# Strassen's seven products in the last down projection of a two-block transformer kernel

## Chip, cores and metric

One Trainium2 chip, one of its cores. The time is device microseconds of one execution of the whole program, median of several runs; lower is better.

## What is computed

The reference is a two-layer transformer block (attention, convolutional feed-forward, layer norms) followed by a second block with two branches (attention and a state-space scan). All in float32, 512 tokens, width 1024. The change touches only the last feed-forward of the second block, width `D_FF_2` = 2816:

```
gate, up = jnp.split(h2 @ w_gate_up[i], 2, axis=-1)
ffn = (jax.nn.silu(gate) * up) @ w_down[i]
x = x + rms_norm(ffn, norm2_post[i])
```

The output is x, 512 x 1024.

## The kernel before

Every float32 matrix product is made of three products of a reduced type (`F32R`): each operand is split into a rounded part and the rest (`hi`, `lo`), and hi x hi, hi x lo and lo x hi are summed in PSUM. A split is one ScalarE copy (L185 or L193) and one VectorE subtraction (L186 or L194). `wchunk` does it for weights: a DMA of 512 KB on SP's queue into one of 3 raw tiles, then whi and wlo in one of 4 buffers each.

The last feed-forward, `ffn2`, keeps the normalized input transposed (`xTh`, `xTl`, 8 tiles of 128 rows by 512 tokens). `w_in(g)` computes group g of eleven: 256 columns of gate and of up, as two pairs of products (`ws_pairs`, L217 to L219), each 24 matmuls of 512 columns into one bank of the PSUM pool `mm` (3 banks; `at` has 4). ScalarE takes the Silu of gate (L1410), VectorE multiplies with up (L1411), and the result, 128 hidden units by 512 tokens, is split into `hh` and `hl`, so that hidden units lie on partitions.

The down projection (`xs`, L257 to L259) uses these as the stationary operand: for each of 4 row blocks t (128 tokens) and each half c of the 1024 output columns it sums over hidden tiles. It is done in two parts, as 12 pairs of `hh` and `hl` are kept: groups 0 to 5 by `w_in`, then hidden tiles 0 to 10 into `acc` by ScalarE (`first`), then groups 6 to 10 and tiles 11 to 21 (`second`). `second` adds to `acc` (L1425), takes the mean square on ScalarE (L1429), multiplies with the norm's gain (L1430); with the second half it forms 1/sqrt by a power on GpSimd (`rstd2`, L1385), scales and adds x on VectorE (L1435) and stores the rows from SP's queue (L1436). In the last column half the four last weight chunks are loaded ahead (`stagger`), so that the row blocks end one after the other.

The order of the instructions on each engine is set at build time by a scheduler in the framework; each engine then works in that order, and waits by semaphores.

Of the kernel before, what the change touches and what calls it, by code (L numbers as in the profile page):

```python
# [8 lines left out]
F32 = mybir.dt.float32  # L9
F32R = mybir.dt.float32r  # L10
AF = mybir.ActivationFunctionType
ALU = mybir.AluOpType
# [3 lines left out]
S = 512  # L16
D = 1024
P = 128
KD = D // P
NT = S // P  # L20
# [60 lines left out]
class K:  # L81
# [1297 lines left out]
    def rstd2(self, ss, eps=RMS_EPS):  # L1379
# [5 lines left out]
        nc.gpsimd.tensor_tensor(out=r, in0=v, in1=self.mhalf[:, :1], op=ALU.pow)  # L1385
        return r

    def to_T2(self, src, t):
        for half in range(2):
            pt = self.psa()  # L1390
            for j in range(4):
                self.nc.tensor.transpose(pt[:, j * P:(j + 1) * P], src[half][:, j * P:(j + 1) * P], self.ident)
            sl = slice(t * P, (t + 1) * P)
            self.split(pt.rearrange("p (j c) -> p j c", j=4), self.xTh[:, half * 4:half * 4 + 4, sl], self.xTl[:, half * 4:half * 4 + 4, sl])

    def ffn2(self, pool):
        nc, I = self.nc, self.I
        W1, W2 = I["w_gate_up_2"][0], I["w_down_2"][0]
        G = self.bcast(I["norm2_post_2"][0], "G", pool)
        x = pool.tile([P, NT, D], F32, name="x2")  # L1400
        acc = pool.tile([P, NT, D], F32, name="acc")
        xd = self.xd.rearrange("(t p) d -> t p d", p=P)
        hT = {}

        def w_in(g):
            gc = self.ws_load(W1, g * 256)
            uc = self.ws_load(W1, DFF + g * 256)
            for i, gp, up in self.ws_pairs(gc, uc, g == 0):
                sg = pool.tile([P, S], F32, tag="cy", name="cy", bufs=3)
                nc.scalar.activation(sg, gp, AF.Silu)  # L1410
                nc.vector.tensor_tensor(out=sg, in0=up, in1=sg, op=ALU.mult)  # L1411
                hT[g * 2 + i] = (pool.tile([P, S], F32R, tag="hh", name="hh", bufs=12), pool.tile([P, S], F32R, tag="hl", name="hl", bufs=12))
                self.split(sg, *hT[g * 2 + i])

        def first(c):
            return lambda t, ps: nc.scalar.activation(acc[:, t, c * 512:(c + 1) * 512], ps, AF.Copy)

        sst = [self.sm.tile([P, 2], F32, tag="ss3", name="ss3") for _ in range(NT)]
        ags = {}

        def second(c):
            def epi(t, ps):
                sl = slice(c * 512, (c + 1) * 512)
                a = acc[:, t, sl]
                nc.vector.tensor_tensor(out=a, in0=ps, in1=a, op=ALU.add)  # L1425
                jk = pool.tile([P, 512], F32, tag="jk", name="jk")
                ag = pool.tile([P, 512], F32, tag="ag", name="ag", bufs=6)
                ags[t, c] = ag
                nc.scalar.activation(jk, a, AF.Square, scale=1.0 / 32, accum_out=sst[t][:, c:c + 1])  # L1429
                nc.vector.tensor_tensor(out=ag, in0=a, in1=G[:, sl], op=ALU.mult)  # L1430
                if c == 1:
                    r = self.rstd2(sst[t])
                    for i in range(2):
                        sl = slice(i * 512, (i + 1) * 512)
                        nc.vector.scalar_tensor_tensor(out=x[:, t, sl], in0=ags[t, i], scalar=r, in1=x[:, t, sl], op0=ALU.mult, op1=ALU.add)  # L1435
                        nc.sync.dma_start(self.out[t * P:(t + 1) * P, sl], x[:, t, sl])  # L1436
            return epi

        for g in range(6):
            w_in(g)  # L1440
        for t in range(NT):
            nc.scalar.dma_start(x[:, t, :], xd[t])
        for k0, epi, st in ((0, first, 0), (11, second, 4)):
            if k0:
                for g in range(6, 11):
                    w_in(g)
            for c in range(2):
                self.xs(W2, c * 512, 512, 11, lambda k: hT[k0 + k][0], lambda k: hT[k0 + k][1], epi(c), stagger=st if c else 0, k0=k0)

    def run(self):  # L1450
        nc, I, tc = self.nc, self.I, self.tc
# [72 lines left out]
```

## Time and profile before

| | |
|---|---|
| median of 3 runs | 2114.72 us (2114.29 to 2115.11) |
| profiled execution: its time | 2114.72 us |
| profiled execution: its span, first to last instruction | 2112.5 us |
| mean granted TensorE clock | 0.997 of full speed |
| TensorE, VectorE, ScalarE, GpSimd busy | 98%, 62%, 48%, 3% |

In the rows PE is TensorE (PEld its weight loads), DVE VectorE, ACT ScalarE, POOL GpSimd, SP the queue from which most DMAs are issued. L186 is line 186. Up to L1386 the lines of both kernels are the same; of later ones L1392, L1410, L1411, L1416, L1425, L1429, L1430, L1435 and L1436 belong to the kernel before, and L1397 to L1400, L1413, L1438 to L1482, L1507, L1508 and L1523 to L1534 to the changed one. A listed matmul overlaps the next one: its duration is not what one costs. A row of a timeline gives start, duration, engine, line, operation, output and input, count, and in brackets the idle time before it and what ended it.

### The profile page before, as it was taken

How to read it: one execution, taken by the hardware profiler on the slowest of the kernel's cores; microseconds unless marked ns; L12 is line 12 of the kernel's file. 1: busy time of each engine (PE TensorE's matmuls, PEld its weight loads, DVE VectorE, ACT ScalarE, POOL GpSimd, SP SyncE). 2: the span in 40 equal slices, each digit the busy share in tenths (PEclk: the TensorE clock that was granted, in tenths of full speed). 3: DMA queues.
4: the chain of work that ended last, by engine and by line, in shares of the span. 5: the costliest groups of instructions: out<-in, count | busy, mean ns of one | idle time of the engine just before them, and what ended most of it. 6: DMA issues, size and time to landing. Idle time of an engine off the chain costs nothing.

```text
span 2112.5 us, 27971 instructions
## 1 busy us (share of the span) xinstructions
PE 2068.1 (98%) x10707; PEld 1749.6 (83%) x10707; DVE 1312.0 (62%) x2466; ACT 1018.7 (48%) x1856; POOL 72.5 (3%) x109
## 2 busy tenths in 40 slices
PE   8999999999999999999999998999999999999998
PEld 7888888888888789888888887887898878888887
DVE  6777876535636888775536547897798554332334
ACT  4777554324425977444324434676575343223222
POOL 0000000000000000110000001000000010000000
PEclk9999999999999999999999999999999999999999
DMA  6221233232323121162323333211323425232322
GB/s 168 61 61 61 71 122 116 91 99 80 110 79 100 61 70 61 52 166 84 105 85 111 94 100 98 70 31 35 105 61 90 149 94 176 80 105 89 116 90 70
DMA packets 197563, 193.70 MB, mean 92 GB/s; under 512 B 9029, under 2 KB 170550, under 8 KB 197430
## 3 DMA queue, kind: packets, MB, share of 16 engines
q1 hardware_dynamic: 191494, 173.04, 27.4%
q0 software_dynamic: 4928, 15.22, 2.4%
q10 hardware_dynamic: 1008, 3.67, 0.5%
q8 instruction: 84, 1.38, 0.3%
q14 instruction: 49, 0.40, 0.1%
HBM read 185.61 MB, written 6.29 MB: 91 GB/s over the span
## 4 chain that ended last, share of the span: by engine, by line
PE 51%; DVE 3%; ACT 1%; issue 1%; POOL 1%; POOLq 0%; DVEq 0%; ACTq 0%
PE mm L217 10%; PE mm L218 10%; PE mm L219 10%; PE mm L258 2%; PE mm L257 2%; PE mm L259 2%; PE at L257 2%; PE at L259 2%; PE at L258 2%; PE mm L292 1%; PE mm L293 1%; PE mm L291 1%; PE at L1184 1%; PE at L401 1%; DVE wlo L186 1%
## 5 line engine op out<-in xcount | busy, mean ns | idle before, releaser
L186 DVE TENSOR_TENSOR wlo<-raw,whi 128x1024 fp32r<-128x1024 f32 (+3 forms) x336 | 397.6, 1185 | 337.8 <-ACT whi L185 332.0
L217 PE MATMUL mm<-xTh,whi 128*128 128x512 f32 (+1 forms) x1584 | 605.1, 382 | 0.2 <-ACT xTh L193 0.2
L219 PE MATMUL mm<-xTh,wlo 128*128 128x512 f32 (+1 forms) x1584 | 604.3, 382 | 0.1
L218 PE MATMUL mm<-xTl,whi 128*128 128x512 f32 (+1 forms) x1584 | 604.3, 382 | 0.0
L185 ACT ACTIVATE whi<-raw 128x1024 fp32r<-128x1024 f32 (+3 forms) x336 | 345.2, 1031 | 492.7 <-PE at L259 227.2
L219 PEld LDWEIGHTS mm<-xTh,wlo 128*128 128x128 f32 x1584 | 298.3, 188 | 55.9 <-DVE wlo L186 0.3
L217 PEld LDWEIGHTS mm<-xTh,whi 128*128 128x128 f32 x1584 | 298.4, 188 | 55.0 <-ACT xTh L193 0.5
L218 PEld LDWEIGHTS mm<-xTl,whi 128*128 128x128 f32 x1584 | 298.7, 189 | 54.5 <-DVE xTl L194 0.2
L838 DVE SCALAR_TENSOR_TENSOR cy<-mm,cols,cy 128x511 f32<-128x511 f32 (+1 forms) x172 | 128.5, 747 | 107.7 <-ACT cy L836 104.8
L292 PE MATMUL mm<-wlo,xTh 128*128 128x256 f32 x416 | 117.8, 284 | 0.8 <-DVE wlo L186 0.8
L291 PE MATMUL mm<-whi,xTh 128*128 128x256 f32 x416 | 118.1, 285 | 0.3 <-ACT xTh L193 0.3
L293 PE MATMUL mm<-whi,xTl 128*128 128x256 f32 x416 | 117.5, 283 | 0.2 <-DVE xTl L194 0.2
L257 PE MATMUL mm<-whi,hh 128*128 128x512 f32 x264 | 102.9, 390 | 0.0
L257 PE MATMUL at<-whi,hh 128*128 128x512 f32 x264 | 102.8, 389 | 0.0
L258 PE MATMUL at<-wlo,hh 128*128 128x512 f32 x264 | 102.8, 389 | 0.0
L258 PE MATMUL mm<-wlo,hh 128*128 128x512 f32 x264 | 102.8, 389 | 0.0
L259 PE MATMUL mm<-whi,hl 128*128 128x512 f32 x264 | 102.8, 389 | 0.0
L259 PE MATMUL at<-whi,hl 128*128 128x512 f32 x264 | 102.7, 389 | 0.0
L836 ACT ACTIVATE cy<-mm,cols 128x512 f32<-128x512 f32 x86 | 66.2, 769 | 72.6 <-PE mm L219 72.6
L193 ACT ACTIVATE hh<-cy 128x512 fp32r<-128x512 f32 x66 | 41.1, 623 | 116.5 <-DVE cy L1411 58.9
L193 ACT ACTIVATE ph<-at 128x512 fp32r<-128x512 f32 (+3 forms) x128 | 58.6, 474 | 55.1 <-PE at L401 41.3
L292 PEld LDWEIGHTS mm<-wlo,xTh 128*128 128x128 f32 x416 | 79.4, 191 | 1.9 <-DVE wlo L186 1.0
(416 smaller groups left out, 3432.0 us busy)
## 6 DMA issues: line engine op xcount, KB each, us to landing
raw<-in_ffn_w_in_dram SPq DMA_DIRECT2D x88, 512.0 KB
raw<-in_w_gate_up_dram SPq DMA_DIRECT2D x44, 512.0 KB
raw<-in_ffn_w_out_dram SPq DMA_DIRECT2D x40, 512.0 KB
raw<-in_w_in_dram SPq DMA_DIRECT2D x40, 512.0 KB
raw<-in_a_w_in_dram SPq DMA_DIRECT2D x22, 512.0 KB
raw<-in_w_down_dram SPq DMA_DIRECT2D x20, 512.0 KB
raw<-in_kv_w_dram SPq DMA_DIRECT2D x16, 512.0 KB
raw<-in_a_w_out_dram SPq DMA_DIRECT2D x8, 512.0 KB
```

Source lines behind the costliest of these rows:

```text
L185: nc.scalar.activation(hi, raw, AF.Copy)
L186: nc.vector.tensor_tensor(out=lo, in0=raw, in1=hi.bitcast(F32), op=ALU.subtract)
L217: mm(o, wh, a, start=(k == 0), stop=False)
L218: mm(o, wh, b, start=False, stop=False)
L219: mm(o, wl, a, start=False, stop=(k == ktiles - 1))
L257: mm(o, a, hi[:, kk, :], start=(k == 0), stop=False)
L258: mm(o, a, lo[:, kk, :], start=False, stop=False)
L259: mm(o, b, hi[:, kk, :], start=False, stop=(k == ktiles - 1))
L291: mm(o, a, hi[:, kk, :], start=(k == 0 and t % 2 == 0), stop=False)
L292: mm(o, a, lo[:, kk, :], start=False, stop=False)
L293: mm(o, b, hi[:, kk, :], start=False, stop=(k == ktiles - 1 and t % 2 == 1))
L838: nc.vector.scalar_tensor_tensor(out=y[:, o:], in0=ps[:, :S - o], scalar=self.c1(f"cw{l}{j}", m), in1=y[:, o:], op0=ALU.mult, op1=ALU.add)
```

## The change

Ten of the eleven groups of the down projection go by Strassen's algorithm, in the form of Winograd. Two groups (four hidden tiles) make a phase, `st_phase`. The 512 x 1024 output is a 2 x 2 matrix of blocks of 256 tokens by 512 columns; of each group the hidden tile 0 and 1 are the two halves of the inner dimension. Four blocks of the weight, `b11`, `b12`, `b21`, `b22`, each 128 x 512 for both groups of the phase in one tile of 1024 columns, are loaded unsplit into `wr` (`st_load`). Seven products replace eight: their stationary operands are three of the four blocks of activations and four sums (`st_operands`, VectorE, lines L1397 to L1400, in `R`, split as 256 and 1536 columns), their moving operands `b11`, `b21`, `b22` and four differences formed on GpSimd (L1451, L1452, L1453, L1462), which overwrite `b11`, `b12` and twice `t2`. A product is 12 matmuls of 512 columns (L1438) into two banks, one of each row block, after a split of its weights. The products are added up in `u2`, `u3`, `u5` (VectorE L1464, L1465; ScalarE L1455, L1474) and in `acc`, by VectorE from PSUM (L1471, L1479, L1482) and by GpSimd from SBUF (L1447, L1476). Group 10 goes the usual way (`xsn`), with both column halves of a row block one after the other, and its epilogue ends the program; x is loaded in two buffers instead of four.

```diff
         nc.gpsimd.tensor_tensor(out=r, in0=v, in1=self.mhalf[:, :1], op=ALU.pow)
         return r
 
+    BLOCKS = 7 * 256
+    def st_operands(self, pool, R):
+        tt = self.nc.vector.tensor_tensor
+        b = lambda i: R[:, i * 256:(i + 1) * 256]
+        tt(out=b(4), in0=b(1), in1=b(3), op=ALU.add)
+        tt(out=b(5), in0=b(4), in1=b(0), op=ALU.subtract)
+        tt(out=b(6), in0=b(0), in1=b(1), op=ALU.subtract)
+        tt(out=b(7), in0=b(2), in1=b(5), op=ALU.subtract)
+        hi = pool.tile([P, self.BLOCKS], F32R, tag="hh", name="hh", bufs=3)
+        lo = pool.tile([P, self.BLOCKS], F32R, tag="hl", name="hl", bufs=3)
+        self.split(R[:, 0:256], hi[:, 0:256], lo[:, 0:256])
+        self.split(R[:, 512:2048], hi[:, 256:], lo[:, 256:])
+        return hi, lo
+    def st_load(self, pool, W, g, bufs):
+        Wv = W.rearrange("(g i p) (j c) -> i j p g c", i=2, p=P, j=2)
+        B = {}
+        for i, j in ((0, 0), (0, 1), (1, 1), (1, 0)):
+            B[i, j] = pool.tile([P, 1024], F32, tag="wr", name="wr", bufs=bufs)
+            self.nc.sync.dma_start(B[i, j].rearrange("p (g c) -> p g c", g=2), Wv[i, j][:, g:g + 2, :])
+        return B
+    def wsplit(self, raw):
+        hi = self.wp.tile([P, 1024], F32R, tag="whi", name="whi", bufs=4)
+        lo = self.wp.tile([P, 1024], F32R, tag="wlo", name="wlo", bufs=4)
+        self.split(raw, hi, lo)
+        return hi, lo
+    def st_phase(self, pool, B, hs, acc, first, bufs):
+        nc = self.nc
+        mm = nc.tensor.matmul
+        T = nc.gpsimd.tensor_tensor
+        b11, b12, b21, b22 = B[0, 0], B[0, 1], B[1, 0], B[1, 1]
+        def product(block, raw, bank):
+            w = self.wsplit(raw)
+            ps = [bank(), bank()]
+            for p in range(2):
+                h, l = hs[p]
+                for t in range(2):
+                    a = h[:, block * 256 + t * P:block * 256 + (t + 1) * P]
+                    b = l[:, block * 256 + t * P:block * 256 + (t + 1) * P]
+                    wh, wl = (x[:, p * 512:(p + 1) * 512] for x in w)
+                    mm(ps[t], a, wh, start=p == 0, stop=False)
+                    mm(ps[t], a, wl, start=False, stop=False)
+                    mm(ps[t], b, wh, start=False, stop=p == 1)
+            return ps
+        U = lambda: pool.tile([P, 1024], F32, tag="U", name="U", bufs=3)
+        half = lambda x, t: x[:, t * 512:(t + 1) * 512]
+        ac = lambda i, j, t: acc[:, 2 * i + t, j * 512:(j + 1) * 512]
+        V = nc.vector.tensor_tensor
+        add = lambda out, a: T(out=out, in0=out, in1=a, op=ALU.add)
+        t2 = pool.tile([P, 1024], F32, tag="wr", name="wr", bufs=bufs)
+        u2, u3, u5 = U(), U(), U()
+        ps = product(0, b11, self.psa)
+        T(out=b11, in0=b12, in1=b11, op=ALU.subtract)
+        T(out=b12, in0=b22, in1=b12, op=ALU.subtract)
+        T(out=t2, in0=b22, in1=b11, op=ALU.subtract)
+        for t in range(2):
+            nc.scalar.activation(half(u2, t), ps[t], AF.Copy)
+            if first:
+                nc.scalar.activation(ac(0, 0, t), ps[t], AF.Copy)
+            else:
+                add(ac(0, 0, t), half(u2, t))
+        p7 = product(5, b12, self.psa)
+        ps = product(4, t2, self.psum)
+        T(out=t2, in0=t2, in1=b21, op=ALU.subtract)
+        for t in range(2):
+            V(out=half(u2, t), in0=ps[t], in1=half(u2, t), op=ALU.add)
+            V(out=half(u3, t), in0=p7[t], in1=half(u2, t), op=ALU.add)
+            if not first:
+                for i, j, u in ((1, 1, u3), (0, 1, u2), (1, 0, u3)):
+                    add(ac(i, j, t), half(u, t))
+        ps = product(1, b21, self.psa)
+        for t in range(2):
+            V(out=ac(0, 0, t), in0=ps[t], in1=ac(0, 0, t), op=ALU.add)
+        ps = product(3, b11, self.psa)
+        for t in range(2):
+            nc.scalar.activation(half(u5, t), ps[t], AF.Copy)
+            for i, u in ((1, u3), (0, u2)):
+                T(out=ac(i, 1, t), in0=half(u, t) if first else ac(i, 1, t), in1=half(u5, t), op=ALU.add)
+        ps = product(6, b22, self.psum)
+        for t in range(2):
+            V(out=ac(0, 1, t), in0=ps[t], in1=ac(0, 1, t), op=ALU.add)
+        ps = product(2, t2, self.psa)
+        for t in range(2):
+            V(out=ac(1, 0, t), in0=half(u3, t) if first else ac(1, 0, t), in1=ps[t], op=ALU.subtract)
     def to_T2(self, src, t):
         for half in range(2):
             pt = self.psa()
...
@@ -1397,55 +1493,58 @@
         nc, I = self.nc, self.I
         W1, W2 = I["w_gate_up_2"][0], I["w_down_2"][0]
         G = self.bcast(I["norm2_post_2"][0], "G", pool)
-        x = pool.tile([P, NT, D], F32, name="x2")
         acc = pool.tile([P, NT, D], F32, name="acc")
         xd = self.xd.rearrange("(t p) d -> t p d", p=P)
-        hT = {}
+        hs, B = {}, {}
+        WR = 7
 
         def w_in(g):
             gc = self.ws_load(W1, g * 256)
             uc = self.ws_load(W1, DFF + g * 256)
+            R = pool.tile([P, 2048], F32, tag="R", name="R", bufs=2)
             for i, gp, up in self.ws_pairs(gc, uc, g == 0):
-                sg = pool.tile([P, S], F32, tag="cy", name="cy", bufs=3)
+                sg = R[:, i * 512:(i + 1) * 512]
                 nc.scalar.activation(sg, gp, AF.Silu)
                 nc.vector.tensor_tensor(out=sg, in0=up, in1=sg, op=ALU.mult)
-                hT[g * 2 + i] = (pool.tile([P, S], F32R, tag="hh", name="hh", bufs=12), pool.tile([P, S], F32R, tag="hl", name="hl", bufs=12))
-                self.split(sg, *hT[g * 2 + i])
-
-        def first(c):
-            return lambda t, ps: nc.scalar.activation(acc[:, t, c * 512:(c + 1) * 512], ps, AF.Copy)
+            if g < 10:
+                hs[g] = self.st_operands(pool, R)
+            else:
+                hs[g] = [pool.tile([P, self.BLOCKS], F32R, tag=n, name=n, bufs=3)[:, :1024] for n in ("hh", "hl")]
+                self.split(R[:, :1024], *hs[g])
 
         sst = [self.sm.tile([P, 2], F32, tag="ss3", name="ss3") for _ in range(NT)]
-        ags = {}
-
-        def second(c):
+
+        def last(c):
+            sl = slice(c * 512, (c + 1) * 512)
+
             def epi(t, ps):
-                sl = slice(c * 512, (c + 1) * 512)
+                if c == 0:
+                    xt[t] = pool.tile([P, D], F32, tag="x2", name="x2", bufs=2)
+                    nc.scalar.dma_start(xt[t], xd[t])
                 a = acc[:, t, sl]
                 nc.vector.tensor_tensor(out=a, in0=ps, in1=a, op=ALU.add)
-                jk = pool.tile([P, 512], F32, tag="jk", name="jk")
-                ag = pool.tile([P, 512], F32, tag="ag", name="ag", bufs=6)
-                ags[t, c] = ag
+                jk = pool.tile([P, 1024], F32, tag="U", name="U", bufs=3)[:, :512]
                 nc.scalar.activation(jk, a, AF.Square, scale=1.0 / 32, accum_out=sst[t][:, c:c + 1])
-                nc.vector.tensor_tensor(out=ag, in0=a, in1=G[:, sl], op=ALU.mult)
+                nc.vector.tensor_tensor(out=a, in0=a, in1=G[:, sl], op=ALU.mult)
                 if c == 1:
                     r = self.rstd2(sst[t])
                     for i in range(2):
-                        sl = slice(i * 512, (i + 1) * 512)
-                        nc.vector.scalar_tensor_tensor(out=x[:, t, sl], in0=ags[t, i], scalar=r, in1=x[:, t, sl], op0=ALU.mult, op1=ALU.add)
-                        nc.sync.dma_start(self.out[t * P:(t + 1) * P, sl], x[:, t, sl])
+                        s = slice(i * 512, (i + 1) * 512)
+                        nc.vector.scalar_tensor_tensor(out=xt[t][:, s], in0=acc[:, t, s], scalar=r, in1=xt[t][:, s], op0=ALU.mult, op1=ALU.add)
+                        nc.sync.dma_start(self.out[t * P:(t + 1) * P, s], xt[t][:, s])
             return epi
 
-        for g in range(6):
-            w_in(g)
-        for t in range(NT):
-            nc.scalar.dma_start(x[:, t, :], xd[t])
-        for k0, epi, st in ((0, first, 0), (11, second, 4)):
-            if k0:
-                for g in range(6, 11):
-                    w_in(g)
-            for c in range(2):
-                self.xs(W2, c * 512, 512, 11, lambda k: hT[k0 + k][0], lambda k: hT[k0 + k][1], epi(c), stagger=st if c else 0, k0=k0)
+        xt = {}
+        w_in(0)
+        w_in(1)
+        for g in range(0, 10, 2):
+            B = self.st_load(pool, W2, g, WR)
+            w_in(g + 2)
+            self.st_phase(pool, B, (hs[g], hs[g + 1]), acc, g == 0, WR)
+            if g < 8:
+                w_in(g + 3)
+        h, l = hs[10]
+        self.xsn([(W2, c * 512, last(c)) for c in range(2)], 2, lambda k: h[:, k * 512:(k + 1) * 512], lambda k: l[:, k * 512:(k + 1) * 512], 20)
 
     def run(self):
         nc, I, tc = self.nc, self.I, self.tc
```

What the scheduler made of it, at three places. **VectorE in the down projection.** Before, after the last gate and up (`cy`), it stands at the splits of the weights (`wlo`) alone:

```order
L1411 TENSOR_TENSOR cy_17980<-mm_17931,cy_17980 128x512
L186 TENSOR_TENSOR wlo_18083<-raw_18081,whi_18082 128x1024
L194 TENSOR_TENSOR hl_17984<-cy_17980,hh_17983 128x512
L186 TENSOR_TENSOR wlo_18113<-raw_18111,whi_18112 128x1024
L186 TENSOR_TENSOR wlo_18143<-raw_18141,whi_18142 128x512
L186 TENSOR_TENSOR wlo_18181<-raw_18179,whi_18180 128x1024
L186 TENSOR_TENSOR wlo_18215<-raw_18213,whi_18214 128x1024
```

Now, in a middle phase (groups 4 and 5), from the first sum of group 6, which is computed just ahead and is used by the next phase, two rows behind the split of `t2`, to the second of the two `u3` (`U_17425`; `U_17424` is `u2`; `wlo_17500` belongs to `b21`, `wlo_17520` to `b11` the second time, `wlo_17544` to `b22`):

```order
L1397 TENSOR_TENSOR R_17308<-R_17308 128x256
L194 TENSOR_TENSOR wlo_17500<-wr_17282,whi_17499 128x1024
L1398 TENSOR_TENSOR R_17308<-R_17308 128x256
L1400 TENSOR_TENSOR R_17308<-R_17308 128x256
L194 TENSOR_TENSOR hl_17418<-R_17308,hh_17417 128x1536
L194 TENSOR_TENSOR wlo_17520<-wr_17276,whi_17519 128x1024
L1464 TENSOR_TENSOR U_17424<-mm_17474,U_17424 128x512
L194 TENSOR_TENSOR wlo_17544<-wr_17280,whi_17543 128x1024
L1465 TENSOR_TENSOR U_17425<-at_17456,U_17424 128x512
L1464 TENSOR_TENSOR U_17424<-mm_17475,U_17424 128x512
L1471 TENSOR_TENSOR acc_15997<-at_17503,acc_15997 128x512
L1465 TENSOR_TENSOR U_17425<-at_17457,U_17424 128x512
```

Sums, a split of 1536 columns and three splits of weights stand between TensorE's third product (`mm_17474`) and the reading of the second product's banks (`at_17456`, `at_17457`), into which the fifth product goes.

**GpSimd over the whole last feed-forward.** Before, between the load of the gain and the end there is nothing but the four powers:

```order
L1385 TENSOR_TENSOR ss_15969<-ss_15968,mhalf 128x1
L353 DMA G<-in_norm_post_dram 128x1024
L1385 TENSOR_TENSOR ss_18294<-ss_18293,mhalf 128x1
L1385 TENSOR_TENSOR ss_18328<-ss_18327,mhalf 128x1
L1385 TENSOR_TENSOR ss_18362<-ss_18361,mhalf 128x1
L1385 TENSOR_TENSOR ss_18396<-ss_18395,mhalf 128x1
```

Now, from that load through the first phase and the second, after which two more phases read as the second one does, and the last too:

```order
L353 DMA G<-in_norm_post_dram 128x1024
L1451 TENSOR_TENSOR wr<-wr 128x1024
L1452 TENSOR_TENSOR wr<-wr 128x1024
L1453 TENSOR_TENSOR wr<-wr 128x1024
L1462 TENSOR_TENSOR wr<-wr 128x1024
L1476 TENSOR_TENSOR acc<-U 128x512 x4
L1451 TENSOR_TENSOR wr<-wr 128x1024
L1452 TENSOR_TENSOR wr<-wr 128x1024
L1453 TENSOR_TENSOR wr<-wr 128x1024
L1462 TENSOR_TENSOR wr<-wr 128x1024
L1447 TENSOR_TENSOR acc<-acc,U 128x512 x8
L1476 TENSOR_TENSOR acc<-acc,U 128x512 x4
```

Each phase has four subtractions of 1024 columns and, from the second on, twelve additions of 512.

**VectorE at the end.** Before, each row block had its own five instructions:

```order
L1425 TENSOR_TENSOR acc_15998<-mm_18199,acc_15998 128x512
L1430 TENSOR_TENSOR ag_18358<-acc_15998,G_15995 128x512
L1384 SCALAR_TENSOR_TENSOR ss5_18361<-ss3_16001 128x1
L1435 SCALAR_TENSOR_TENSOR x2_15997<-ag_18171,ss6_18362,x2_15997 128x512
L1435 SCALAR_TENSOR_TENSOR x2_15997<-ag_18358,ss6_18362,x2_15997 128x512
L1425 TENSOR_TENSOR acc_15998<-at_18206,acc_15998 128x512
L1430 TENSOR_TENSOR ag_18392<-acc_15998,G_15995 128x512
L1384 SCALAR_TENSOR_TENSOR ss5_18395<-ss3_16002 128x1
L1435 SCALAR_TENSOR_TENSOR x2_15997<-ag_18176,ss6_18396,x2_15997 128x512
L1435 SCALAR_TENSOR_TENSOR x2_15997<-ag_18392,ss6_18396,x2_15997 128x512
```

Now, from the scaling of row block 1 to the end, the additions of the matmuls of row blocks 2 and 3 stand together, and all multiplications and scalings behind them:

```order
L1533 SCALAR_TENSOR_TENSOR x2_18520<-acc_15997,ss6_18538,x2_18520 128x512 x2
L1528 TENSOR_TENSOR acc_15997<-acc_15997,G_15995 128x512
L1525 TENSOR_TENSOR acc_15997<-mm_18558,acc_15997 128x512
L1525 TENSOR_TENSOR acc_15997<-mm_18577,acc_15997 128x512
L1525 TENSOR_TENSOR acc_15997<-mm_18590,acc_15997 128x512
L1528 TENSOR_TENSOR acc_15997<-acc_15997,G_15995 128x512
L1384 SCALAR_TENSOR_TENSOR ss5_18569<-ss3_16000 128x1
L1528 TENSOR_TENSOR acc_15997<-acc_15997,G_15995 128x512
L1533 SCALAR_TENSOR_TENSOR x2_18552<-acc_15997,ss6_18570,x2_18552 128x512 x2
L1528 TENSOR_TENSOR acc_15997<-acc_15997,G_15995 128x512
L1384 SCALAR_TENSOR_TENSOR ss5_18601<-ss3_16001 128x1
L1533 SCALAR_TENSOR_TENSOR x2_18584<-acc_15997,ss6_18602,x2_18584 128x512 x2
```

The rows of before lay 21 matmuls of TensorE apart, those of the change 12.

## Rows read from the trace of the kernel before

**Rows 1.** The page, part 1: busy time, share, instructions of each engine.

```profile
span 2112.5 us, 27971 instructions
PE 2068.1 (98%) x10707; PEld 1749.6 (83%) x10707; DVE 1312.0 (62%) x2466; ACT 1018.7 (48%) x1856; POOL 72.5 (3%) x109
```

**Rows 2.** Busy time of each engine in two stretches: us, then busy (instructions).

```profile
core 0: us, PE busy (x) PEld busy (x) DVE busy (x) ACT busy (x) POOL busy (x), PEclk, DMA share, GB/s
1941.50:1963.30 21.80, 21.80 (x98) 18.06 (x97) 7.58 (x8) 6.48 (x8) 0.00 (x0) 1.00 0.35 106
...
2072.00:2112.50 40.50, 32.87 (x145) 26.79 (x144) 20.91 (x32) 9.58 (x20) 2.21 (x4) 0.94 0.17 61
```

**Rows 3.** Groups by line from 1750 us on: count, total, mean ns.

```profile
L186 DVE TENSOR_TENSOR wlo<-raw,whi 128x1024 fp32r<-128x1024 f32 x60 | 73.5, 1225 | 102.2 <-ACT whi L185 102.0
...
L257 PE MATMUL mm<-whi,hh 128*128 128x512 f32 x132 | 51.4, 389 | 0.0
...
L257 PE MATMUL at<-whi,hh 128*128 128x512 f32 x44 | 17.1, 389 | 0.0
```

**Rows 4.** Timeline, TensorE, inside a group: start, duration.

```profile
1962.80 0.39 PE L218 MATMUL mm<-xTl,whi 128*128 128x512 f32 x1
...
1965.97 0.39 PE L217 MATMUL mm<-xTh,whi 128*128 128x512 f32 x1
```

**Rows 5.** Timeline, VectorE, close instructions.

```profile
2073.54 1.22 DVE L186 TENSOR_TENSOR wlo<-raw,whi 128x1024 fp32r<-128x1024 f32 x1
2074.67 0.69 DVE L1430 TENSOR_TENSOR ag<-acc,G 128x512 f32<-128x512 f32 x1
2075.28 1.28 DVE L1425 TENSOR_TENSOR acc<-mm,acc 128x512 f32<-128x512 f32 x2
```

**Rows 6.** Timeline, ScalarE, close instructions.

```profile
1903.61 1.06 ACT L185 ACTIVATE whi<-raw 128x1024 fp32r<-128x1024 f32 x1 [4.38 <-PE at L259]
1904.58 1.67 ACT L1416 ACTIVATE acc<-mm 128x512 f32<-128x512 f32 x3
```

**Rows 7.** Timelines of VectorE and GpSimd: powers alone and beside VectorE.

```profile
1735.58 0.68 DVE L194 TENSOR_TENSOR xTl<-at,xTh 128x512 fp32r<-128x512 f32 x1
1735.81 0.55 POOL L1385 TENSOR_TENSOR ss<-ss,mhalf 128x1 f32<-128x1 f32 x1 [2.88 <-DVE ss L1384]
1740.73 1.22 DVE L186 TENSOR_TENSOR wlo<-raw,whi 128x1024 fp32r<-128x1024 f32 x1
1740.96 1.41 POOL L1385 TENSOR_TENSOR ss<-ss,mhalf 128x1 f32<-128x1 f32 x1 [2.32 <-DVE ss L1384]
...
1291.93 1.64 POOL L363 TENSOR_TENSOR rs<-rs,mhalf 128x8 f32<-128x8 f32 x1 [6.34 <-DVE rs L362]
1298.35 1.01 POOL L363 TENSOR_TENSOR rs<-rs,mhalf 128x4 f32<-128x4 f32 x1 [4.78 <-DVE rs L362]
```

**Rows 8.** Timeline of the end: row block 2, the last matmul, row block 3.

```profile
2100.15 0.69 DVE L1425 TENSOR_TENSOR acc<-mm,acc 128x512 f32<-128x512 f32 x1 [0.92 <-PE mm L259]
...
2104.49 0.39 PE L259 MATMUL at<-whi,hl 128*128 128x512 f32 x1
2104.91 0.69 DVE L1425 TENSOR_TENSOR acc<-at,acc 128x512 f32<-128x512 f32 x1 [0.91 <-PE at L259]
2105.64 0.69 DVE L1430 TENSOR_TENSOR ag<-acc,G 128x512 f32<-128x512 f32 x1
...
2106.45 0.16 DVE L1384 SCALAR_TENSOR_TENSOR ss<-ss 128x1 f32<-128x1 f32 x1
2106.76 0.55 POOL L1385 TENSOR_TENSOR ss<-ss,mhalf 128x1 f32<-128x1 f32 x1 [4.21 <-DVE ss L1384]
2107.34 1.41 DVE L1435 SCALAR_TENSOR_TENSOR x<-ag,ss,x 128x512 f32<-128x512 f32 x2 [0.73 <-POOL ss L1385]
```

**Rows 9.** DMA issues: KB each, median us to landing.

```profile
xd<-x POOLq DMA_DIRECT2D x4, 512.0 KB, 3.0
...
xd<-L POOLq DMA_DIRECT2D x8, 256.0 KB, 2.5
```

## The prediction

> **What bounds the kernel now.** I read the page's busy shares first: TensorE is busy for 98% of the span, VectorE for 62%, GpSimd for 3% [rows 1]. Then the busy time by stretch: while a group of the last feed-forward is computed TensorE is busy in all of the 21.80 us and VectorE in 7.58; the last 40.50 us hold the only idle TensorE time of this stage [rows 2]. Then the groups by line, for how many matmuls of the down projection there are and what a split of weights costs [rows 3], and the timeline for how closely instructions follow each other. Fourteen matmuls of 512 columns start 3.17 us after the first [rows 4], and the 21 matmuls between two epilogues of the end take 4.76 us, so one costs 0.2267 us, though each is listed with 0.39. So TensorE sets the time; a matmul saved is worth 0.2267 us where its operands are there, and only there.
>
> A difference under 0.2% (4.2 us) counts as no change here, about what a measurement of this kernel can tell.
>
> **What the change removes.** The down projection has (132+44)x3 = 528 matmuls [rows 3]. Now it has 5 phases of 7 products of 12 (420) and 48 for the last group, 468. 60 x 0.2267 = 13.6 us less on TensorE. That is the whole gain.
>
> **What it costs, prices first.** VectorE takes 1.13 us per 1024 columns and 0.60 per 512 where instructions follow closely (0.33 and 1.67 for 256 and 1536 by the same slope), and the result is there after 1.22 and 0.69 [rows 5]; an instruction that reads what the one before it wrote starts 0.13 later than that [rows 8]. ScalarE: 1.06 until the result for 1024, 0.53 per 512 [rows 6]; 1.49 for 1536 by the same slope. The new work on GpSimd has no row: it has only run powers of 1 to 8 columns. Lower end: VectorE's pace, 1.13 and 0.60 us, since nothing shows GpSimd faster anywhere. Upper end: one column costs it 0.55 us where VectorE takes 0.16 [rows 7, 8], 3.4 times as much: 3.85 and 2.05 us. (Its powers cost 0.16 us more per further column [rows 7], 160 us for 1024; a power is another arithmetic and I leave that out.) VectorE's subtraction of the same tile is the nearest row, so I take a low multiple of it, twice: 2.26 us for 1024 columns and 1.2 for 512. The Trainium skill (GPSIMD Engine Reference, "Performance versus the Vector engine") has 4497 ns against VectorE's 2293 for an fp32 add of 2048 columns; by that ratio of 1.96 the sum would be lower by under 3 us. No run here shows it.
>
> **A lock between GpSimd and VectorE.** A power of one column takes 0.55 us while VectorE subtracts with one operand in PSUM, but 1.41 when it starts 0.23 us into a weight split, whose two operands both lie in SBUF [rows 7]: it ends 0.42 us after the split. So GpSimd stood still for it. The other direction, VectorE held up by GpSimd, no row shows: it costs between nothing and the whole rest of a GpSimd instruction. I take the whole rest, since what keeps one side out for a full instruction of the other is nearest to something that one of them has at a time. The Trainium skill (SBUF — State Buffer, "Who interferes with whom") says that whichever of the two starts first holds the shared port and the other fully blocks. By that rule, with which [rows 7] agrees in the one direction, the sum is the one with both directions, and it speaks against the change, which puts 20 wide and 52 narrow GpSimd instructions beside VectorE's splits.
>
> **A middle phase (three of five), t = 0 where TensorE comes to its first product.** The order of the instructions is that of the fences above; I add 0.04 us from one engine to the next.
> 1. The four weight buffers come free in steps of 12 matmuls, the first 8.16 us ahead. ScalarE (1.06) and VectorE (1.22) split b11 until -5.6. GpSimd's three subtractions follow each other: -3.3, -1.0, 1.3. ScalarE has t2 rounded at 2.36; VectorE, in order, starts its split at 2.40 and is free at 3.53.
> 2. Behind it stand on VectorE: the product of gate and up (0.60, and 0.13 for the reader behind it), the sum L1397, the split of b21, L1398 and L1400: done at 6.60. ScalarE rounds 1536 columns until 8.13, VectorE subtracts them until 9.84; then b11's second split (1.13), u2 (0.60), b22's split (1.13), u3 (0.69): 13.39. The second u3 is done at 15.19.
> 3. TensorE is at its fifth product at 48 x 0.2267 = 10.88. That needs the two PSUM banks of product two (the pool has four), which these two u3 read last. It waits 2.5 us for the first, and after three matmuls 1.1 for the second: **3.7 us** without any lock.
> 4. With the lock L1397 waits for GpSimd's fourth subtraction (3.66 to 5.92), 1.66 us, and L1400 for its first addition, 1.07 us. All behind shifts by 2.73: 16.12 and 17.92, a wait of 6.4 us.
> 5. VectorE's L1479 waits for the last of GpSimd's 12 additions, which by their number and the lock end at 30.8. Behind it stands the split of the next up weights, done at 32.7; TensorE wants it at 31.3. 1.4 us more: **7.8 us**.
>
> The first phase has no additions ahead of L1400 and another order of the two u3: 2.0 us, and 1.7 of the lock (L1397 again): **3.7 us**.
>
> **Last phase and end.** VectorE stands at L1479 until GpSimd's last addition at 28.2 (21.5 without lock) and has done the phase's last sum at 30.2; unhindered, TensorE would end the phase at 19.0 and the last group at 29.9, and 7.6 us behind the last matmul [rows 8] would be 37.5. But the 48 matmuls now take 2.7 us per row block where they left 4.76, and VectorE does all eight epilogues in a row: 8 L1525 and 8 L1528 of 0.60, 8 L1533 of 0.70, four short ones of 0.08, 0.8 for the first Square, 0.7 for the last power, 3.7 from the last L1533 to the end [rows 8]: 20.7 us. 30.2 + 20.7 = 50.9, so **13.4 us** later.
>
> **At nothing:** 15 more weight splits (35 for 20) on ScalarE, whose b21 is rounded at 3.3 for a use at 8.16; were they late, each would cost up to 1.06 us. The weights' bytes are the same and their loads are issued a group (21.8 us) ahead, at a DMA share of 0.35 [rows 2]. The loads of the next phase stand ahead of one raw load in SP's queue until b11's second split, at 13.8; that raw load waits for its own buffer until 21.4 anyway. In ScalarE's queue the last two loads of x wait for stores: 2.5 us to land, 3.0 for the load [rows 9] and 0.4 to issue, 5.9 behind the store of two blocks earlier, which VectorE needs 8 us later; a slower load would add its excess to the end.
>
> **Sum, likeliest case:** -13.6 + 3.7 + 3 x 7.8 + 13.4 = +26.9 us. The profiled execution has a span of 2112.5 and a time of 2114.72, which is also the median of the three runs: **2141.6 us**, 1.3% slower. With 1.95 or 2.6 us for the wide subtraction the same steps give +14 and +43, 2129 to 2157.
>
> **Rivals.**
> - A, the lock does not hold VectorE. Then waits are 2.0, 3 x 4.4 and 10.6 where GpSimd still waits (+12.2, 2126.9), or 2.0, 3 x 3.7 and 6.6 with no lock at all (+6.1, 2120.8). For it: only one direction has rows. Against: that one is clear.
> - B, faster: GpSimd subtracts at about VectorE's pace. The three subtractions then end at -2.1, t2's split is no longer what VectorE stands behind, and the waits shrink to 0, 3 x 1.3 and 3.2 even with the lock: -6.5, 2108.2; without the lock 0.5 each and 3.1, -9.0, 2105.7. It decides below 1.4 us per wide subtraction with the lock, below 1.95 without. For it: the additions are as simple as VectorE's. Against: 0.55 us for one column.
> - C, GpSimd at the upper end: waits of 12.3, 3 x 23.9 and 29.9, +100 us, 2215 (without lock +57, 2172).
> - That the change removes less than it says is no rival: the built program has 60 matmuls fewer.
>
> **How the numbers follow.** 0.48 for the forecast, as one bound price is taken from a neighbour's row; 0.2 for A, 0.22 for B, 0.1 for C. Faster by over 0.2% is B but for the part near its threshold, 0.18. Within 0.2%: that part and the quick end of A, 0.1. Slower 0.72. The range leaves out C and the faster half of B: 2110 to 2158; the forecast's own range is 2129 to 2157.
>
> **What would show it.** Right: in the waits of the changed kernel the fifth product (L1438, into the `at` banks) waits for VectorE's L1465, 4 to 7 us in a middle phase; splits and L1397 on VectorE listed longer than 1.22 and 0.42 or idle ahead while GpSimd runs; GpSimd's 128x1024 subtraction near 2.3 us; TensorE's last matmul some 12 us ahead of the end instead of 7.6, since the last row block waits for VectorE to read a bank. Wrong: L1438 with next to no idle ahead of it, a subtraction of 1.1 us (B), or VectorE's splits at 1.22 us amid GpSimd's work (A).

## Result and profile after

| | before | changed |
|---|---|---|
| median | 2114.60 us (2114.29 to 2115.11, 4 runs) | 2150.22 us (2147.92 to 2151.74, 4 runs) |
| profiled execution: time, span | [rows 1] | 2147.92, 2146.1 us |
| mean granted clock | 0.997 | 0.991 |

The ratio is 1.0167 (95% interval 1.015 to 1.0185, in brackets further on): 35.6 us slower. The spans of the two profiled executions differ by 33.6 us; the profiled one is the fastest of the four of the changed kernel, and what follows explains its span. The page's busy time, to be read against [rows 1]:

```profile
PE 2067.4 (96%) x10647; PEld 1743.0 (81%) x10647; DVE 1414.1 (66%) x2568; ACT 1046.2 (49%) x1882; POOL 208.4 (10%) x181
```

TensorE has fewer matmuls and 96% where it had 98. The waits of TensorE from 1800 us on (what it waited for: us in total, times, longest) say where it stands:

```profile
PE at L1438 <- DVE U L1465: 23.7, 5, 6.0
PE mm L637 <- DVE acc L1479: 1.9, 2, 1.1
PE at L1438 <- ACT acc L1457: 1.6, 1, 1.6
PE at L1439 <- DVE wlo L194: 1.0, 3, 0.3
PE mm L637 <- DVE acc L1525: 1.0, 1, 1.0
```

The first line is the fifth product of each phase, waiting for the sums u3 to leave its banks. In the second phase, whose first product starts at 1877.53, GpSimd's timeline is

```profile
1871.80 2.39 POOL L1451 TENSOR_TENSOR wr<-wr 128x1024 f32<-128x1024 f32 x1 [35.29 <-DVE wlo L194]
1874.27 2.40 POOL L1452 TENSOR_TENSOR wr<-wr 128x1024 f32<-128x1024 f32 x1
1876.62 2.41 POOL L1453 TENSOR_TENSOR wr<-wr 128x1024 f32<-128x1024 f32 x1
1881.46 2.40 POOL L1462 TENSOR_TENSOR wr<-wr 128x1024 f32<-128x1024 f32 x1 [2.43 <-DVE wlo L194]
...
1895.53 1.27 POOL L1447 TENSOR_TENSOR acc<-acc,U 128x512 f32<-128x512 f32 x1
1896.77 1.27 POOL L1447 TENSOR_TENSOR acc<-acc,U 128x512 f32<-128x512 f32 x1
1898.01 2.26 POOL L1447 TENSOR_TENSOR acc<-acc,U 128x512 f32<-128x512 f32 x1
```

and VectorE's, over the same time:

```profile
1877.79 3.59 DVE L194 TENSOR_TENSOR wlo<-wr,whi 128x1024 fp32r<-128x1024 f32 x2 [6.07 <-ACT whi L193]
1881.30 0.68 DVE L1508 TENSOR_TENSOR R<-mm,R 128x512 f32<-128x512 f32 x1
1882.02 2.12 DVE L1397 TENSOR_TENSOR R<-R 128x256 f32<-128x256 f32 x1
1884.06 2.30 DVE L194 TENSOR_TENSOR wlo<-wr,whi 128x1024 fp32r<-128x1024 f32 x1
1886.29 1.50 DVE L1398 TENSOR_TENSOR R<-R 128x256 f32<-128x256 f32 x1
...
1894.35 0.68 DVE L1465 TENSOR_TENSOR U<-at,U 128x512 f32<-128x512 f32 x1
1894.95 0.68 DVE L1464 TENSOR_TENSOR U<-mm,U 128x512 f32<-128x512 f32 x1
1895.55 0.68 DVE L1471 TENSOR_TENSOR acc<-at,acc 128x512 f32<-128x512 f32 x1
1896.15 0.68 DVE L1465 TENSOR_TENSOR U<-at,U 128x512 f32<-128x512 f32 x1
1896.75 0.68 DVE L1471 TENSOR_TENSOR acc<-at,acc 128x512 f32<-128x512 f32 x1
1897.35 1.78 DVE L194 TENSOR_TENSOR wlo<-wr,whi 128x1024 fp32r<-128x1024 f32 x1
```

Two things are to be seen. L1397, 256 columns that take 0.42 us elsewhere, lasts 2.12 and ends at 1884.14, just behind GpSimd's L1462 (1883.86): VectorE stood. The split of `b21` behind it (2.30 us for 1.22) and L1398 (1.50 for 0.42) meet GpSimd's first additions; in the first phase, which has no additions there, the same two take 1.21 and 0.41. And the five instructions from 1894.35 to 1897.4 have an operand in PSUM; they keep their 0.6 us pace beside GpSimd's additions, and these keep 1.27. Where the next split reads SBUF twice, both sides stretch (1.78 and 2.26). TensorE at that moment:

```profile
1888.82 0.39 PE L1440 MATMUL at<-whi,hl 128*128 128x512 f32 x1
1895.18 0.77 PE L1438 MATMUL at<-whi,hh 128*128 128x512 f32 x1 [5.97 <-DVE U L1465]
1895.74 0.63 PE L1439 MATMUL at<-wlo,hh 128*128 128x512 f32 x1
1896.17 0.63 PE L1440 MATMUL at<-whi,hl 128*128 128x512 f32 x1
```

Behind the wait matmuls follow each other at 0.427 us, not 0.2267. The windows of the wait, of the stretch behind it and of what follows (the columns as in [rows 2]; PEclk is the last number but two) show the granted clock at half, the 1.2 GHz level, for 12 matmuls, then whole again:

```profile
1888.90:1895.10 6.20, 0.31 (x2) 0.00 (x0) 5.29 (x6) 4.66 (x5) 1.72 (x1) 0.90 0.05 19
1895.20:1900.40 5.20, 5.20 (x12) 4.04 (x13) 5.20 (x6) 0.60 (x1) 5.20 (x5) 0.50 0.00 0
1902.00:1918.00 16.00, 16.00 (x72) 13.26 (x71) 6.97 (x9) 3.06 (x5) 7.73 (x6) 1.00 0.44 132
```

At the end GpSimd's last four additions hold VectorE, its epilogues then follow in a row, and the last load of x comes late:

```profile
2117.39 5.00 POOL L1476 TENSOR_TENSOR acc<-acc,U 128x512 f32<-128x512 f32 x4
```

```profile
2119.95 0.69 DVE L1479 TENSOR_TENSOR acc<-mm,acc 128x512 f32<-128x512 f32 x1 [3.67 <-POOL acc L1476]
2123.03 1.27 DVE L1482 TENSOR_TENSOR acc<-acc,at 128x512 f32<-128x512 f32 x2
...
2140.93 1.42 DVE L1533 SCALAR_TENSOR_TENSOR x<-acc,ss,x 128x512 f32<-128x512 f32 x2 [1.57 <-DMA x<-xd]
```

The last matmul starts at 2133.00, 13.1 us ahead of the end, where 8.0 were before ([rows 8], and the span). The phases' first products start at 1810.80, 1877.53, 1949.54, 2021.39 and 2093.28 us; there are 276 matmuls from one to the next (62.6 us at 0.2267) and 131 from the last of these starts to the last matmul. What lies above that is the measured term (the end is 13.1 us against 8.0):

| term | forecast | measured |
|---|---|---|
| 60 matmuls saved | -13.6 | -13.6 |
| first phase | 3.7 | 4.2 |
| three middle phases | 3 x 7.8 = 23.4 | 9.4 + 9.3 + 9.3 = 28.0 |
| last phase and end | 13.4 | 10.0 + 5.1 = 15.1 |
| sum | 26.9 | 33.7, for 33.6 |

### The profile page after: what moved, and what is told of

It is laid out like the page before. It is cut to its first block, busy times and chain, and to the rows that moved or that the text cites. A ratio compares the mean times of both kernels' runs of the same rounds, so it can differ in the third digit from the quotient of the medians.

```text
span 2146.1 us, 28099 instructions
## 1 busy us (share of the span) xinstructions
PE 2067.4 (96%) x10647; PEld 1743.0 (81%) x10647; DVE 1414.1 (66%) x2568; ACT 1046.2 (49%) x1882; POOL 208.4 (10%) x181
## 3 DMA queue, kind: packets, MB, share of 16 engines
q1 hardware_dynamic: 191462, 173.04, 26.9%
## 4 chain that ended last, share of the span: by engine, by line
PE 34%; issue 11%; DVE 5%; POOL 5%; ACT 2%; DMA 1%; DVEq 0%; POOLq 0%; SPq 0%; ACTq 0%
PE mm L217 7%; PE mm L219 7%; PE mm L218 7%; POOL acc L1447 1%; PE at L257 1%; PE at L259 1%; PE at L258 1%; POOL acc L1476 1%; DVE wlo L194 1%; PE mm L259 1%; PE mm L257 1%; PE mm L258 1%; PE mm L292 1%; PE mm L293 1%; PE mm L291 1%
## 5 line engine op out<-in xcount | busy, mean ns | idle before, releaser
L186 DVE TENSOR_TENSOR wlo<-raw,whi 128x1024 fp32r<-128x1024 f32 (+3 forms) x314 | 380.3, 1213 | 252.0 <-ACT whi L185 246.3
L185 ACT ACTIVATE whi<-raw 128x1024 fp32r<-128x1024 f32 (+3 forms) x314 | 323.6, 1035 | 410.0 <-PE mm L218 193.2
L1385 POOL TENSOR_TENSOR ss<-ss,mhalf 128x1 f32<-128x1 f32 x36 | 22.0, 613 | 859.4 <-DVE ss L1384 856.8
L258 PE MATMUL at<-wlo,hh 128*128 128x512 f32 x220 | 85.7, 390 | 0.0
L257 PE MATMUL at<-whi,hh 128*128 128x512 f32 x220 | 85.7, 389 | 0.0
L259 PE MATMUL at<-whi,hl 128*128 128x512 f32 x220 | 85.6, 389 | 0.0
L194 DVE TENSOR_TENSOR wlo<-wr,whi 128x1024 fp32r<-128x1024 f32 x35 | 56.7, 1623 | 41.4 <-ACT whi L193 41.1
L291 PEld LDWEIGHTS mm<-whi,xTh 128*128 128x128 f32 x416 | 79.8, 192 | 1.5 <-ACT xTh L193 0.7
L293 PEld LDWEIGHTS mm<-whi,xTl 128*128 128x128 f32 x416 | 79.9, 192 | 1.1 <-DVE xTl L194 0.6
```

The source lines that it names most:

```text
L185: nc.scalar.activation(hi, raw, AF.Copy)
L186: nc.vector.tensor_tensor(out=lo, in0=raw, in1=hi.bitcast(F32), op=ALU.subtract)
L257: mm(o, a, hi[:, kk, :], start=(k == 0), stop=False)
L258: mm(o, a, lo[:, kk, :], start=False, stop=False)
L259: mm(o, b, hi[:, kk, :], start=False, stop=(k == ktiles - 1))
L291: mm(o, a, hi[:, kk, :], start=(k == 0 and t % 2 == 0), stop=False)
```

## Experiments

All compare with runs of the kernel before on the same chip (medians of 2115.0 to 2115.6 us).

**1. The differences early, still on GpSimd.** In `st_load`, behind the loads; `st_phase` uses B[0] to B[2] where it formed them.

```diff
+        T = self.nc.gpsimd.tensor_tensor
+        for k in range(3):
+            B[k] = pool.tile([P, 1024], F32, tag="wr", name="wr", bufs=bufs)
+        T(out=B[0], in0=B[0, 1], in1=B[0, 0], op=ALU.subtract)
...
-        T(out=b11, in0=b12, in1=b11, op=ALU.subtract)
```

> The four weight differences stay on GpSimd, but go into tiles of their own as soon as the weights are loaded, not over b11 and t2 after their splits. VectorE's order is unchanged. Theory (GpSimd's chain and its lock make VectorE late for L1465): t2's split is no longer late and L1397 meets no subtraction, so the fifth product waits under 2 us instead of 6, TensorE's slow stretch behind that wait goes too, and GpSimd's additions end some 4 us earlier: 2124 us (2118 to 2130). Rival (VectorE's queue ahead of L1465 is too long in itself): the wait stays at 5 us or more, 2145.

Measured: 2159.32 us, 1.0202 [1.0187, 1.0218], slower than the change. TensorE's waits from 1760 us on:

```profile
PE mm L219 <- DVE wlo L186: 16.2, 5, 3.8
PE mm L217 <- DVE acc L1482: 9.8, 3, 3.3
PE at L1445 <- DVE U L1468: 5.1, 3, 1.7
```

The fifth product (L1445 here) does wait 1.7 us only, as the theory said. But the next phase's differences (L1417 to L1420) now need only loaded weights and free buffers, and the scheduler put them between this phase's additions (L1454, L1479):

```profile
1896.42 2.39 POOL L1418 TENSOR_TENSOR wr<-wr 128x1024 f32<-128x1024 f32 x1
1898.77 3.39 POOL L1419 TENSOR_TENSOR wr<-wr 128x1024 f32<-128x1024 f32 x1
1902.12 8.24 POOL L1454 TENSOR_TENSOR acc<-acc,U 128x512 f32<-128x512 f32 x5
1910.32 4.93 POOL L1479 TENSOR_TENSOR acc<-acc,U 128x512 f32<-128x512 f32 x4
1915.22 2.34 POOL L1420 TENSOR_TENSOR wr<-wr 128x1024 f32<-128x1024 f32 x1
```

The additions end at 1915.25, and VectorE's last sums and the up-weight splits behind them come later still: 3.3 and 3.8 us, with slow matmuls behind. The expectation (2118 to 2130) failed: it missed the order on GpSimd. The wait went to where step 5 of the forecast had put its 1.4 us.

**2. The differences on VectorE.** All four, in the change's place.

```diff
-        T(out=b11, in0=b12, in1=b11, op=ALU.subtract)
+        V(out=b11, in0=b12, in1=b11, op=ALU.subtract)
...
```

> The four weight differences go to VectorE (1.13 us each for 2.39), in the same place; the additions stay on GpSimd. Theory: the chain to t2's split is 3 us shorter, no subtraction locks L1397; the fifth product waits 0 to 1.5 us, and GpSimd's last additions then hold L1479 and the up-weight split behind it for 2 to 3 us: 2124 us (2118 to 2132). Rival (VectorE's own load): 4.5 us more per phase on VectorE make the wait 8 us and more, 2155 or above.

Measured: 2127.42 us, 1.0052 [1.0037, 1.0067], in the range. The fifth product (L1439 here) waits 2.0 us, above the 0 to 1.5 expected, but 4 us less than in the change though VectorE has more to do; the additions' wait appears, and the rival falls:

```profile
PE at L1439 <- DVE U L1465: 5.9, 3, 2.0
PE mm L219 <- DVE wlo L186: 5.5, 3, 1.8
PE mm L637 <- DVE acc L1479: 3.5, 2, 2.8
```

**3. The additions on VectorE.** L1447 and L1476.

```diff
-        add = lambda out, a: T(out=out, in0=out, in1=a, op=ALU.add)
+        add = lambda out, a: V(out=out, in0=out, in1=a, op=ALU.add)
...
```

> The twelve additions to acc per phase go to VectorE, the four differences stay on GpSimd. Theory: t2's split and L1397 are as late as before, so the fifth product still waits 4 to 6 us and TensorE still runs slow behind it; only what L1479 waited for at the end goes, some 5 us: 2140 us (2132 to 2148). Rival (the additions on GpSimd are what costs): the wait goes, 2120.

Measured: 2143.41 us, 1.013 [1.0115, 1.0145]. The fifth product still waits, up to 4.5 us, and the clock still falls behind it:

```profile
PE at L1438 <- DVE U L1465: 18.3, 5, 4.5
```

So the differences are the larger part, by both runs: 23 us of the change's time go with them, 7 with the additions. How much of the 23 is GpSimd's slowness and how much the lock, these runs don't separate.

**4. Sums apart.** The products are linear in the phases, so each can be summed over them and combined once.

```diff
+        def into(k, ps):
+            for t in range(2):
+                o = acc[:, k, t * 512:(t + 1) * 512]
+                if first:
+                    nc.scalar.activation(o, ps[t], AF.Copy)
+                else:
+                    nc.vector.tensor_tensor(out=o, in0=ps[t], in1=o, op=ALU.add)
+
+        into(0, product(0, b11, self.psa))
...
-        for g in range(0, 10, 2):
+        for g in range(0, 8, 2):
...
+            if g == 6:
+                self.st_end(acc)
+        w_in(10)
...
+            self.xs(W2, c * 512, 512, 6, xh(0), xh(1), last(c), stagger=3 * c, k0=16)
```

> Strassen for eight groups, three the usual way; each of the seven products is summed over the phases in a tile of its own (14 sums per phase, VectorE, from PSUM), combined once behind the last phase, and the differences are formed early on VectorE: GpSimd has no work. 48 matmuls saved, 10.9 us. Theory (GpSimd and the order behind it cost all the rest): waits under 1 us each, the end as before: 2106 us (2103 to 2111). Rival (a phase has too much for VectorE in 19 us, whoever helps): 2118 or more.

Measured: 2109.07 us, 0.9971 [0.9961, 0.9981]: 0.3% faster than the kernel before. TensorE waits at one place only, 0.6 and 1.3 us, for the up weights beside the first phase's differences: VectorE, in order, stood at a difference whose weights were still being loaded. The run changes four things at once: where products are combined, the engine and the place of the differences, the number of phases, and the order of the last groups (`xs`, one column half after the other). No run has eight groups with the differences and the additions both on VectorE and the products still combined in every phase, so what the sums apart are worth by themselves stays open.

**5. The same, differences on GpSimd.**

```diff
-        T = self.nc.vector.tensor_tensor
+        T = self.nc.gpsimd.tensor_tensor
```

> The kernel with sums apart, but its four differences per phase on GpSimd (2.4 us each for VectorE's 1.13), early, while up weights are split. GpSimd still locks those splits. Theory (GpSimd's slowness and lock cost only where somebody waits for what stands behind them; a group of 21.8 us leaves VectorE some 8 us): splits listed at 2 us and more, but no new wait of TensorE above 1 us, and the first phase's wait of 1.9 us goes because VectorE no longer stands at a load: 2107 us (2104 to 2111). Rival (each lock reaches TensorE): some 2.4 us per difference, 2120 or more.

Measured: 2109.21 us, 0.9971 [0.9959, 0.9982]. The groups by line, 1780 to 2060 and 1740 to 2060 us:

```profile
L186 DVE TENSOR_TENSOR wlo<-raw,whi 128x1024 fp32r<-128x1024 f32 x38 | 56.2, 1490 | 28.2 <-ACT whi L185 28.1
```

```profile
L1417 POOL TENSOR_TENSOR wr<-wr 128x1024 f32<-128x1024 f32 x4 | 14.0, 3502 | 148.2 <-DVE wlo L194 139.7 <-DMA wr<-in_w_down_dram 8.5
```

GpSimd now needs 3.1 to 3.5 us (means of the four lines; the slowest is shown) for what VectorE does in 1.13, and lengthens the splits (1.22 to 1.49 on average), yet the time is that of run 4: no phase but the first has a wait. There it is 2.3 us instead of 1.9; the expectation had it gone. Here slowness and lock cost only what somebody waits for.

**6. Tuned.** The first phase's differences on GpSimd, the gain's product in a tile of its own.

```diff
-                nc.vector.tensor_tensor(out=a, in0=a, in1=G[:, sl], op=ALU.mult)
+                ag = acc[:, 2 + t // 2 * 2, t % 2 * 512:(t % 2 + 1) * 512] if c else a
+                ags[t, c] = ag
+                nc.vector.tensor_tensor(out=ag, in0=a, in1=G[:, sl], op=ALU.mult)
```

> The kernel with sums apart, with the first phase's differences on GpSimd and the product with the norm's gain of the second column half in a tile of its own, so that VectorE no longer waits 0.85 us for each of the last Squares. Theory: 1.9 us less at the first phase and about 1 us less at the end: 2106 us (2103 to 2109). Rival (both waits are covered by the next one): as the kernel with sums apart, 2109.

Measured: 2108.68 us, 0.9968 [0.9956, 0.998], not told from run 4. The end did come nearer (8.7 us behind the last matmul instead of 9.5); the first phase's wait did not go: it is 2.3 us, as in run 5, with 8 slow matmuls behind it. Beside GpSimd's first two differences two up-weight splits last 6.5 us:

```profile
1766.71 6.47 DVE L186 TENSOR_TENSOR wlo<-raw,whi 128x1024 fp32r<-128x1024 f32 x2 [0.22 <-ACT whi L185]
```

**7. Ten groups.** As run 4, with five phases and group 10 alone behind them.

> The kernel with sums apart, but ten groups by Strassen as in the change, and only group 10 behind the last phase: 12 matmuls fewer than with eight groups (2.7 us). Theory (with so little for TensorE behind the last phase, its combining and eight epilogues run in a row on VectorE, whatever GpSimd does): waits of TensorE at the last group of some 7 us, the end 8 to 10 us later against TensorE's work: 2114 us (2110 to 2118). Rival (the long end came from GpSimd's additions alone): 2106.

Measured: 2118.30 us, 1.0014 [1.0006, 1.0023], just outside the range and 9.2 us behind run 4 with 12 matmuls fewer. GpSimd has none of the sums here, and yet TensorE waits 5.4 us for a split that stands behind seven combinations on VectorE, with slow matmuls behind it, and the end comes 13.3 us after the last matmul, 1.7 of them for the load of x:

```profile
PE mm L638 <- DVE wlo L186: 5.4, 1, 5.4
```

```profile
2084.67 4.29 DVE L1473 TENSOR_TENSOR acc<-acc 128x512 f32<-128x512 f32 x7
2088.88 2.35 DVE L186 TENSOR_TENSOR wlo<-raw,whi 128x1024 fp32r<-128x1024 f32 x2
...
2110.52 1.42 DVE L1525 SCALAR_TENSOR_TENSOR x<-acc,ss,x 128x512 f32<-128x512 f32 x2 [1.66 <-DMA x<-xd]
```

**8. The change with eight groups.** The last phase goes; three groups follow the usual way, one column half after the other (`xs`), where the change has one group with both halves of a row block together.

```diff
-        for g in range(0, 10, 2):
+        for g in range(0, 8, 2):
...
+        w_in(10)
+        xh = lambda i: lambda k: hs[8 + k // 2][i][:, k % 2 * 512:(k % 2 + 1) * 512]
+        for c in range(2):
+            self.xs(W2, c * 512, 512, 6, xh(0), xh(1), last(c), stagger=3 * c, k0=16)
```

> The change itself, GpSimd's work and all, but eight groups by Strassen and three the usual way behind them: four phases, 48 matmuls saved instead of 60. Theory (the last phase and the end are a term of their own: too little for TensorE stands behind them): the first phase and three middle ones cost 4 and 9.4 us each as before, the end returns to that of the kernel before: -10.9 + 4 + 3 x 9.4 + 1 = 2137 us (2133 to 2141). Rival (the end is late because every phase is late, or it costs as much wherever it stands): 2147 or more.

Measured: 2135.15 us, 1.0095 [1.0079, 1.011]: 15 us less than the change, with 12 more matmuls. The last matmul is 9.2 us ahead of the end. The phases' waits are as before (6.0, 6.0, and 3.9 in the last, beside which no sums of operands are formed). By the distances the first phase costs 5.7 us (here 8 slow matmuls follow its second wait), the two middle ones 9.3 each, the last 6.2 and the end 1.2; 4, 3 x 9.4 and 1 were expected. So the time agrees in part because the first and the last phase were off in opposite directions.

**9. First phase in place.** The tuned kernel, with the first phase's differences on VectorE where the change has them.

```diff
+        if first:
+            T = nc.vector.tensor_tensor
+            t1, t2 = b11, pool.tile([P, 1024], F32, tag="wr", name="wr", bufs=bufs)
+            t3 = t2
+            T(out=t1, in0=b12, in1=b11, op=ALU.subtract)
...
```

> The tuned kernel with sums apart, with the first phase's four differences on VectorE behind the split of b11, where the change has them, so that none stands beside or ahead of the first up-weight splits. Theory (the first differences make the one wait that is left, 2.3 us and the slow stretch behind it): no wait of TensorE in the whole stage, 2106 us (2103 to 2108). Rival (that wait is the four loads of 512 KB ahead of the up weights in the same queue): 2108 to 2109 as now.

Measured: 2105.50 us (2103.79 to 2106.09), 0.9951 [0.9938, 0.9963], the best of all. No wait of TensorE is left in this stage. The four loads stand in the queue as before, so the rival falls: it was the differences beside the splits. The two splits that took 6.5 us in run 6 are back at 1.23 each:

```profile
1766.29 1.23 DVE L186 TENSOR_TENSOR wlo<-raw,whi 128x1024 fp32r<-128x1024 f32 x1 [0.21 <-ACT whi L185]
1767.72 1.23 DVE L186 TENSOR_TENSOR wlo<-raw,whi 128x1024 fp32r<-128x1024 f32 x1 [0.21 <-ACT whi L185]
```

The windows of two phases and of the end:

```profile
1866.00:1930.00 64.00, 64.00 (x284) 52.97 (x284) 41.67 (x50) 22.72 (x24) 0.00 (x0) 1.00 0.33 99
1930.00:1994.00 64.00, 64.00 (x284) 53.01 (x283) 41.07 (x48) 21.69 (x23) 0.00 (x0) 1.00 0.31 99
2060.00:2102.20 42.20, 34.47 (x153) 28.20 (x151) 23.54 (x34) 9.85 (x21) 2.21 (x4) 0.97 0.28 98
```

TensorE is busy all the time at the full clock, VectorE for 41 to 42 of 64 us: in this form, with 14 sums and four differences, the arithmetic of a phase is not too much for it. The change has 22 additions and four differences per phase; eight more at 0.60 us are 4.8 us, so by this estimate they would fit too, if nobody waited for them.

## Why the prediction was right, and where it was off

- **TensorE sets the time, 0.2267 us a matmul: right.** Run 9 saves 48 matmuls, 10.9 us, and its span is 10.3 us shorter than that of [rows 1].
- **GpSimd's price: right.** 2.39 to 2.41 us for the 2.26 taken, 1.27 to 1.30 for 1.2. The ratio cited from the Trainium skill (GPSIMD Engine Reference, "Performance versus the Vector engine") is 1.96; here it is 2.40 / 1.13 = 2.1 against VectorE's pace, and 2.40 / 1.22 = 1.97 against its listed duration [rows 5].
- **The lock holds both: right.** Rival A falls with L1397's 2.12 us (1.70 more than its 0.42, where step 4 had 1.66). Here every stretched instruction reads SBUF twice, and those with a PSUM operand keep their pace. The rule cited from the Trainium skill (SBUF — State Buffer, "Who interferes with whom") agrees.
- **The fifth product waits for L1465: right in mechanism; that 6.0 us came so near to the 6.4 of step 4 is in part luck.** The forecast had 5.3 us at the first bank and 1.1 at the second; measured are 6.0 at the first and none at the second. The lock held three of VectorE's instructions instead of two (1.70 + 1.08 + 1.08 = 3.9 us for 2.73), and the first u3 is done 17.5 us into the phase for 16.12; and with slow matmuls TensorE came to the second bank 1.4 us behind the first, not 0.7. Runs 2 and 3 show that the differences make most of the wait, run 1 that their place alone takes it from 6.0 to 1.7 us.
- **Step 5, 1.4 us more behind L1479: wrong in this kernel.** The split was later (34.1 us into the phase for 32.7), but TensorE was 9.4 us late where step 4 had 6.4, so the split was in time. In run 2, where a phase is shorter, the same wait appears (1.8 us), and in run 1, where the additions end later (3.3 and 3.8 us).
- **What the sum lacked** is the step that failed: after a wait a matmul was taken at 0.2267 us. The prediction put the cost behind a wait at nothing, without a reason. The 12 matmuls behind it took 0.427 us each at a granted clock of 0.50, 2.4 to 2.7 us more per middle phase. The Trainium skill has the rule (TensorE: Matmul & The Clock Gate, "Part 1: The HAM clock gate") that an idle TensorE falls back to 1.2 GHz; the rows above agree. The fourth product also waited 0.6 us for b21's split, which the lock made late. So a middle phase is 9.3 to 9.4 us instead of 7.8: 6.1 for the bank, 2.4 to 2.7 for the slow matmuls, 0.6 for b21, and nothing for step 5.
- **First phase: right in size, half by another cause.** 1.75 us is a wait for ScalarE's copy L1457, which the sum priced at nothing; L1465 makes 2.15.
- **Last phase and end: right**, 15.1 for 13.4. GpSimd's last addition ends 29.1 us into the phase (28.2 forecast), the last sum is done at 31.0 (30.2); 1.6 us is the load of x, named as an excess that might come. Run 8 shows that it is a term of its own: with three groups behind the last phase, that phase and the end cost 7.4 us. Run 7 shows that it is there, 13.7 us, without GpSimd's sums. The runs that fill the end also order the last groups differently, so that too little work behind the last phase is the cause, and not that order, is likely but not shown.
- **Rivals B and C** fall with GpSimd's 2.4 us. What B claimed, a faster kernel, was reached only with GpSimd off the path that TensorE waits for and more groups at the end, as in runs 4, 5, 6 and 9.

## What to carry to other kernels

A saving on the engine that sets the time is worth its matmuls only if nothing new stands in the queues that feed it: follow the slow engine's result through the in-order queue of the engine behind it, to the bank or buffer that somebody wants. What is linear can be summed over the loop and combined once, where there is slack, instead of in every turn: all kernels here that beat the one before do so, though no run shows that step alone. And leave enough work for the bounding engine behind the last such turn.

## What was not expected of the hardware

A short wait can cost more than itself: 6.0 us of wait were followed by 12 matmuls at the half clock, 2.4 us and more. Waits of 1.8 to 2.4 us were sometimes followed by 8 such matmuls (runs 2 and 6) and sometimes by none (the first phase of the change). Runs 5 and 6 have the same wait of 2.33 us at the same place; behind it the granted clock was 1.00 in the one and 0.50 in the other. So that stretch can't be read off the wait's length alone. GpSimd's subtraction of 1024 columns took 2.4 us in the change, where few splits of VectorE fell beside it, and 3.1 to 3.5 us on average in run 5, beside a run of splits.
